# Gathering masked rows for a cumulative sum at the midpoint: a blind front load for every batch, and chunk code entered where the list begins

## The chip, the cores and the metric

The kernel runs on one core of a Trainium2 chip. The metric is the device time of one execution in microseconds (us). A profiled execution also has a span, which runs from the first to the last recorded instruction; the time is a little longer than the span. Engine names are those of the profile: PE (matrix multiply) with PEld (its weight loads), DVE (vector), ACT (scalar), POOL (GpSimd) and SP (sync). A DMA issued from SP or ACT stands in the profile on a queue called hardware_dynamic, one issued from POOL on the queue software_dynamic; a core has 16 DMA engines.

## What is computed

```python
x: [8, 8192, 512] float32, lengths: [8] int64, w: [512, 512] float32
mask = arange(8192) < lengths[:, None]
cs = cumsum(x * mask, axis=1)
mid = cs[b, lengths[b] // 2, :]          # [8, 512]
out = mid @ w                            # [8, 512]
```

So for batch b the kernel needs the sum of the first min(lengths[b] // 2 + 1, lengths[b]) rows of x[b], and then one small matrix product. The lengths are drawn once and fixed: 1138, 5379, 511, 4113, 1809, 7542, 7716, 1140. The rows to be summed are therefore 570, 2690, 256, 2057, 905, 3772, 3859 and 571, which is 14,680 rows of 2 KB, or 30.1 MB out of the 134 MB of x. The lengths are known only when the kernel runs, so it must build the list of what it loads on the chip.

## The kernel before

Rows are handled in groups of U = 4 neighbours (a "quad", 8 KB in one piece). A list of quads runs over all batches, and 128 quads, one per partition, make a chunk of 1 MB. Summing is a matrix product: a weight tile of 128 x 8 zeros and ones says which batch each partition's row belongs to and whether it lies before the end, and four matmuls per chunk (one per row of the quad, each in its own 32-row band of the array, helper `add`, line 285) add into `s_ps`.

**The load without the list.** For batches 0 and 1 the first 512 rows are loaded blind by SP (`xf`, lines 119 to 122), two DMAs of 1 MB whose source is 128 runs of 8 KB in a row. For batches 6 and 7 the first 128 rows come blind, but at the end (`xb`, line 165). Everything else is on the list.

**The list.** DVE (function `vector`; every operation is recorded on line 184 and waits for the one before it) turns the lengths into where each batch's part of the list begins (`row`), PE spreads that over all partitions (line 299 into `bc_ps`), and DVE compares it with each list place to get the quad's number (`idx`). It does this for the first C1 = 8 chunks first (`table(0, C1)`, mark "idx0") and then for the other 57 (`table(C1, C)`, mark "idx"). C = 65 chunks is the most that any lengths could need. The weights `wf`, `wc`, `wb` follow.

**The gathers.** POOL (function `gpsimd`) issues one indirect DMA per chunk (line 151) into a ring of R = 8 buffers `xt`. The code has one block per possible chunk: a compare-and-branch on the list's length (line 171) and the gather, in upward order. Gather c waits for ACT's zeroing of its buffer (`s_zero`; ACT's line 132 clears all eight, since places beyond the list's end are not written) or, from the ninth on, for PE to be done with the buffer (`s_done`). When the list ends, POOL branches to `gp_tail`, which issues the two `xb` and the four `w` loads on the same queue.

**PE** (function `tensor`) does the front, chunk 0, and then a block per chunk: compare-and-branch (line 347), wait for the chunk's semaphore, four matmuls. At the end of the list it branches to `pe_tail`, whose block lies after the blocks of all 65 chunks: the `xb` matmuls, four matmuls that fold the four bands of `s_ps` and transpose (line 331, `mf_ps`), and 16 with w (line 337, `o_ps`). DVE copies between these. SP and ACT each store two pieces of 8 rows of 512 B.

Two waits set the order between the three kinds of work: PE takes the front in order, ahead of every chunk,

```python
for b in range(FRONT):
    pe.wait_ge(s_front[b], 16)      # line 307
```

and a gather beyond the ring waits for PE (`pool.wait_ge(s_done, c - R + 1)`, line 150).

Of the kernel before, what the change touches and what calls it, by code (L numbers as in the profile page):

```python
# [11 lines left out]
P = 128  # L12
# [3 lines left out]
def kernel(  # L16
# [9 lines left out]

    nc = tc.nc
# [7 lines left out]
    FRONT, BACK = 2, 2  # L35
    R0 = [P * U] * FRONT + [0] * (B - FRONT - BACK) + [P] * BACK
    MOST = B * (S // 2 // U + 1)
    C = -(-MOST // P)
    C1 = 8
    FAR = 1 << 17  # L40
    K = [1 - r // U for r in R0]
    JUMP = [UB + (R0[b + 1] - R0[b]) // U - K[b] for b in range(B - 1)] + [FAR]
# [11 lines left out]
    def sem(name):  # L54
        return tc.alloc_semaphore(name)

    xt = sb("xt", [P, R, U * D])
    xf = sb("xf", [P, FRONT, U, D])
    xb = sb("xb", [P, BACK, D])
# [4 lines left out]
    kk = sb("kk", [1, B])  # L64
    negk = sb("negk", [1, B])
    jump = sb("jump", [1, B])
    row = sb("row", [1, 5 * B])
    qk = sb("qk", [1, B])
    mm_ = sb("mm_", [1, B])
    total = sb("total", [1, 1], I32)  # L70
    ones = sb("ones", [1, P])
    zero = sb("zero", [1, D])
    p_i = sb("p_i", [P, 1], I32)
# [6 lines left out]
    f_i = sb("f_i", [P, U], I32)  # L80
    q = sb("q", [P, C])
# [6 lines left out]
    wf = sb("wf", [P, FRONT, U, B])  # L88
    wb = sb("wb", [P, BACK, B])
    fold_i = sb("fold_i", [P, B], I32)  # L90
    fold_m = sb("fold_m", [P, B], I32)
    fold = sb("fold", [P, B])
    s_sb = sb("s_sb", [P, D])
    mf_sb = sb("mf_sb", [P, KC, B])
# [6 lines left out]
    b2_ps = ps("b2_ps", [P, D])  # L101

    s_full = [sem(f"full{k}") for k in range(R)]
    s_front = [sem(f"front{k}") for k in range(FRONT)]
    s_back = [sem(f"back{k}") for k in range(BACK)]
    s_w = [sem(f"w{k}") for k in range(KC)]
    s_len, s_out, s_pool, s_dve, s_pe, s_done, s_zero = (
        sem(n) for n in ("len", "out", "pool", "dve", "pe", "done", "zero"))

    def engine_body(eng, name):  # L110
        eng.br(f"{name}_0")
        return nc.body(f"{name}_0", valid_engines=[eng.engine])

    END = "gather_end"
    bodies = {}


    def sync(sp):
        sp.dma_start(out=xf[:, 0], in_=x[0, :P * U].rearrange("(p u) d -> p u d", u=U)).then_inc(
            s_front[0], 16)  # L120
        sp.dma_start(out=xf[:, 1], in_=x[1, :P * U].rearrange("(p u) d -> p u d", u=U)).then_inc(
            s_front[1], 16)
        sp.wait_ge(s_dve, marks["out"])
        for j in range(0, 4, 2):
            sp.dma_start(out=out[:, j * P:(j + 1) * P], in_=o_sb[32 * j:32 * j + B]).then_inc(s_out, 16)
        sp.wait_ge(s_out, 64)


    def scalar(act):
        act.dma_start(out=lens[:], in_=lens_words).then_inc(s_len, 16)  # L130
        for k in range(R):
            act.memzero(xt[:, k]).then_inc(s_zero, 1)  # L132
        act.wait_ge(s_dve, marks["out"])
        for j in range(1, 4, 2):
            act.dma_start(out=out[:, j * P:(j + 1) * P], in_=o_sb[32 * j:32 * j + B]).then_inc(s_out, 16)


    def gpsimd(pool):
        pool.iota(rank_i[:], pattern=[[0, 1]], base=0, channel_multiplier=13)
        pool.iota(q_i[:], pattern=[[P, C]], base=0, channel_multiplier=0)  # L140
        pool.iota(p_i[:], pattern=[[0, 1]], base=0, channel_multiplier=1)
        pool.iota(v_i[:], pattern=[[P * U, C], [1, U]], base=U, channel_multiplier=0)
        pool.iota(f_i[:], pattern=[[1, U]], base=0, channel_multiplier=U)
        pool.iota(fold_i[:], pattern=[[-1, B]], base=128, channel_multiplier=1).then_inc(s_pool, 1)

        def gather(c):
            if c < R:
                pool.wait_ge(s_zero, c + 1)
            else:
                pool.wait_ge(s_done, c - R + 1)  # L150
            pool.indirect_dma_start(  # L151
                out=xt[:, c % R], out_offset=None, in_=xu,
                in_offset=bass.IndirectOffsetOnAxis(ap=idx[:, c:c + 1], axis=0),
                bounds_check=B * UB - 1, oob_is_err=False,
            ).then_inc(s_full[c % R], 16)

        n = pool.alloc_register("n_pool")
        pool.wait_ge(s_dve, marks["idx0"])
        gather(0)
        pool.load(n, total[:])  # L160
        pool.wait_ge(s_dve, marks["idx"])
        pool.br("gp_1")
        with nc.body("gp_tail", valid_engines=[pool.engine]):
            for k in range(BACK):
                pool.dma_start(out=xb[:, k], in_=x[B - BACK + k, :P]).then_inc(s_back[k], 16)  # L165
            for k in range(KC):
                pool.dma_start(out=wt[:, k], in_=w[k * P:(k + 1) * P]).then_inc(s_w[k], 16)  # L167
            pool.br(END)
        for c in range(1, C):
            with nc.body(f"gp_{c}", valid_engines=[pool.engine]):  # L170
                pool.br_cmp(n, P * c, f"gp_go{c}", "gp_tail", "IS_GT")  # L171
            with nc.body(f"gp_go{c}", valid_engines=[pool.engine]):
                gather(c)
                pool.br(f"gp_{c + 1}" if c + 1 < C else "gp_tail")
# [5 lines left out]
    def vector(dve):  # L180
# [11 lines left out]

        def runs(values):
            k = 0
            while k < len(values):
                e = k
                while e < len(values) and values[e] == values[k]:
                    e += 1
                yield k, e, values[k]
                k = e  # L200
# [4 lines left out]
        for t, values in ((negk, [-a for a in K]), (kk, K), (jump, JUMP)):  # L205
            for k, e, value in runs(values):
                step(dve.memset, t[:, k:e], float(value))
# [3 lines left out]
        step(ts, out=rank4[:], in0=rank_m[:], scalar1=float(U), scalar2=None, op0=ALU.mult)  # L211
        step(ts, out=q[:], in0=q_i[:], scalar1=rank[:], scalar2=None, op0=ALU.add)
        step(ts, out=z[:, :, B], in0=q[:], scalar1=float(R0[0] // U), scalar2=None, op0=ALU.add)
        dve.wait_ge(s_len, 16)
        step(ts, out=l8[:], in0=lens[:, ::2], scalar1=3, scalar2=None, op0=ALU.logical_shift_right)
        step(tt, out=mm_[:], in0=l8[:], in1=negk[:], op=ALU.max)
        step(dve.tensor_tensor_scan, out=row[:, :B], data0=kk[:], data1=mm_[:], initial=0.0,
             op0=ALU.add, op1=ALU.add)
        step(tt, out=row[:, B:2 * B], in0=jump[:], in1=mm_[:], op=ALU.subtract)
        mark("row")  # L220
        step(ts, out=total[:], in0=row[:, B - 1:B], scalar1=0.0, scalar2=None, op0=ALU.add)
        step(tt, out=qk[:], in0=row[:, :B], in1=mm_[:], op=ALU.subtract)
        dve.wait_ge(s_pe, 1)

        def table(a, e):
            n = e - a
            step(tt, out=ge[:, a:e], in0=q[:, a:e].unsqueeze(2).to_broadcast((P, n, B)),
                 in1=bc_ps[:, :B].unsqueeze(1).to_broadcast((P, n, B)), op=ALU.is_ge)
            step(tt, out=z[:, a:e, :B], in0=ge[:, a:e],
                 in1=bc_ps[:, B:2 * B].unsqueeze(1).to_broadcast((P, n, B)), op=ALU.mult)  # L230
            step(dve.tensor_reduce, out=idx[:, a:e], in_=z[:, a:e], axis=AX.X, op=ALU.add)

        table(0, C1)
        mark("idx0")
        step(ts, out=l2[:], in0=lens[:, ::2], scalar1=1, scalar2=None, op0=ALU.logical_shift_right)
        step(dve.scalar_tensor_tensor, out=row[:, 2 * B:3 * B], in0=l2[:], scalar=1.0,
             in1=lens[:, ::2], op0=ALU.add, op1=ALU.min)
        step(tt, out=row[:, 3 * B:4 * B], in0=qk[:], in1=negk[:], op=ALU.add)
        step(dve.scalar_tensor_tensor, out=row[:, 4 * B:], in0=qk[:], scalar=float(U),
             in1=row[:, 2 * B:3 * B], op0=ALU.mult, op1=ALU.add)  # L240
        mark("row2")
        table(C1, C)
        mark("idx")
        step(dve.memset, wf[:], 0.0)
        step(dve.memset, wb[:], 0.0)
        dve.wait_ge(s_pe, 2)
        for b in range(FRONT):
            step(tt, out=wf[:, b, :, b], in0=f_i[:],
                 in1=b2_ps[:, b:b + 1].to_broadcast((P, U)), op=ALU.is_lt)
        mark("front")  # L250

        def weights(a, e):
            n = e - a
            step(tt, out=ge[:, a:e], in0=q[:, a:e].unsqueeze(2).to_broadcast((P, n, B)),
                 in1=b2_ps[:, B:2 * B].unsqueeze(1).to_broadcast((P, n, B)), op=ALU.is_ge)
            step(tt, out=early[:, a:e].rearrange("p c u b -> p (c u) b"),
                 in0=v4[:, a * U:e * U].unsqueeze(2).to_broadcast((P, n * U, B)),
                 in1=b2_ps[:, 2 * B:3 * B].unsqueeze(1).to_broadcast((P, n * U, B)), op=ALU.is_lt)
            step(tt, out=wc[:, a:e], in0=early[:, a:e],
                 in1=ge[:, a:e].unsqueeze(2).to_broadcast((P, n, U, B)), op=ALU.mult)  # L260

# [10 lines left out]
        for k in range(KC):  # L272
            step(dve.tensor_copy, out=s_sb[:, k * P:(k + 1) * P], in_=s_ps[:, k * P:(k + 1) * P])
# [118 lines left out]
```

## Time and profile before

| | us |
|---|---|
| median of 3 runs (97.08 to 97.84) | 97.16 |
| the profiled execution: its time | 97.31 |
| the profiled execution: its span | 95.5 |
| PE / DVE / ACT / POOL busy | 54.1 / 15.9 / 15.8 / 32.6 |
| one gather's issue on POOL (mean of 27) | 1.03 |
| one zeroing of a buffer on ACT (mean of 8) | 1.9 |
| bytes moved by DMA | 31.26 MB, mean 327 GB/s over the span |

The page has a strip of 40 equal slices (2.39 us each) with a digit for how busy each engine and the 16 DMA engines were, and a strip of GB/s. Further views tell the chain of waits that ended last, what single instructions took, and a timeline. The view of windows gives, for any stretch, the busy time of each engine, the granted PE clock, the share of the 16 DMA engines that was busy, and the rate.

### The profile page before, as it was taken

The numbers are of one execution on the slowest core, as the hardware profiler recorded it, in microseconds if no ns is written. First come the engines' busy times: TensorE is split into PE (matmuls) and PEld (weight loads), VectorE is DVE, ScalarE is ACT, GpSimd is POOL, SyncE is SP. The second block draws the span as 40 slices with busy tenths as digits, with TensorE's granted clock in tenths as the row PEclk, the third lists the DMA queues.
The fourth block names the chain that finished last, engine by engine and source line by source line (L and its number), as shares of the span: only waits on it lengthen the run. The fifth ranks groups of instructions, "written<-read, shape, count | busy, mean of one in ns | idle before, by whom it ended". The sixth has DMA issues, their size and how long they took to land.

```text
span 95.5 us, 890 instructions
## 1 busy us (share of the span) xinstructions
PE 54.1 (57%) x308; PEld 8.8 (9%) x308; DVE 15.9 (17%) x56; ACT 15.8 (17%) x9; POOL 32.6 (34%) x43
## 2 busy tenths in 40 slices
PE   2722792447777618763777477746645776219400
PEld 0122100000000000000000000000000000218100
DVE  3778899200000000000000000000000000042100
ACT  3999999200000000000000000000000000000000
POOL 6004578778444440446144534469100000000000
PEclk9999999995555975579556955597596559755555
DMA  2894799999999999999999999999999995000000
GB/s 31 353 412 120 288 353 374 422 425 429 412 436 429 422 401 436 419 412 432 425 412 425 429 412 422 432 412 419 432 422 415 393 389 208 22 0 3 3 10 0
DMA packets 4730, 31.26 MB, mean 327 GB/s; under 512 B 697, under 2 KB 729, under 8 KB 1113
## 3 DMA queue, kind: packets, MB, share of 16 engines
q0 software_dynamic: 4368, 29.04, 74.5%
q1 hardware_dynamic: 320, 2.11, 5.7%
q8 instruction: 5, 0.08, 0.4%
q14 instruction: 3, 0.02, 0.1%
q10 hardware_dynamic: 34, 0.01, 0.0%
HBM read 31.98 MB, written 0.02 MB: 335 GB/s over the span
## 4 chain that ended last, share of the span: by engine, by line
DMA 53%; ACT 17%; PE 12%; issue 9%; DVE 2%; POOL 1%; ACTq 1%; POOLq 0%; SPq 0%
DMA xt<-in_x_dram,idx 53%; ACT xt L132 15%; PE s_ps L286 8%; PE o_ps L337 2%; PE mf_ps L331 2%; ACT L132 1%; DVE s_sb L184 1%; POOL xt L151 1%; ACTq L130 1%; DVE o_sb L184 0%; POOLq L151 0%; POOLq L171 0%; ACTq L387 0%; SPq L46 0%
## 5 line engine op out<-in xcount | busy, mean ns | idle before, releaser
L286 PE MATMUL s_ps<-xt,wc 128*8 128x512 f32 x216 | 42.5, 877 | 24.1 <-DMA xt<-in_x_dram,idx 24.1
L151 POOL DMA_INDIRECT xt<-in_x_dram,idx x27 | 27.7, 1027 | 33.8 <-PE s_ps L286 23.7
L132 ACT ACTIVATE xt<-xt 128x2048 uint32<-128x2048 uint32 x8 | 14.5, 1895 | 0.0
L184 DVE COPY s_sb<-s_ps 128x128 f32<-128x128 f32 x4 | 1.2, 292 | 66.8 <-PE s_ps L286 66.7
L286 PEld LDWEIGHTS s_ps<-xt,wc 128*8 128x8 f32 x216 | 3.4, 89 | 64.0 <-DMA xt<-in_x_dram,idx 62.0
L286 PE MATMUL s_ps<-xf,wf 128*8 128x512 f32 x16 | 3.6, 1051 | 1.7 <-DVE wf L184 1.7
L293 PE MATMUL s_ps<-zero 1*32 1x512 f32 x8 | 1.9, 1056 | 1.9 <-DVE ones L184 1.9
L331 PE MATMUL mf_ps<-fold,s_sb 128*128 128x8 f32 x8 | 1.7, 338 | 2.0 <-DVE s_sb L184 2.0
L286 PE MATMUL s_ps<-xb,wb 128*8 128x128 f32 x16 | 1.0, 410 | 2.6 <-issue 2.6
L184 DVE TENSOR_TENSOR wc<-early,ge 128x256 f32<-128x256 f32 (+1 forms) x2 | 2.5, 1244 | 0.1
L184 DVE TENSOR_TENSOR early<-v,b_ps 128x256 f32<-128x256 f32 (+1 forms) x2 | 2.5, 1237 | 0.1
L167 POOL DMA_DIRECT2D wt<-in_w_dram x4 | 2.2, 575 | 0.0
L331 PEld LDWEIGHTS mf_ps<-fold,s_sb 128*128 128x128 f32 x8 | 1.9, 322 | 2.2 <-issue 1.3
L337 PE MATMUL o_ps<-wt,mf_sb 128*8 128x128 f32 x32 | 1.9, 416 | 0.0
L303 PE MATMUL b_ps<-row,ones 1*128 1x24 f32 x2 | 0.6, 378 | 2.1 <-DVE row L184 2.1
L132 ACT ACT_TABLE_LOAD x1 | 1.3, 1283 | 1.5 <-SPq L46 1.5
L165 POOL DMA_DIRECT2D xb<-in_x_dram x2 | 1.2, 595 | 0.0
L337 PEld LDWEIGHTS o_ps<-wt,mf_sb 128*8 128x8 f32 x32 | 1.1, 126 | 0.4
L299 PE MATMUL bc_ps<-row,ones 1*128 1x16 f32 x2 | 0.6, 380 | 0.8 <-DVE row L184 0.8
L184 DVE COPY mf_sb<-mf_ps 128x8 f32<-128x8 f32 x4 | 0.7, 167 | 1.8 <-PE mf_ps L331 1.8
L184 DVE TENSOR_REDUCE idx<-z 128x8 int32<-128x72 f32 (+1 forms) x2 | 0.9, 459 | 0.1
L184 DVE TENSOR_TENSOR ge<-q,bc_ps 128x64 f32<-128x64 f32 (+1 forms) x2 | 0.9, 426 | 0.4 <-PE bc_ps L299 0.3
(45 smaller groups left out, 12.4 us busy)
## 6 DMA issues: line engine op xcount, KB each, us to landing
xf<-in_x_dram SPq DMA_DIRECT2D x2, 1024.0 KB, 4.9
wt<-in_w_dram POOLq DMA_DIRECT2D x4, 256.0 KB, 15.6
xb<-in_x_dram POOLq DMA_DIRECT2D x2, 256.0 KB, 15.4
xt<-in_x_dram,idx POOLq DMA_INDIRECT x27, 17.2
out_dram<-o_sb SPq DMA_DIRECT2D x2, 4.0 KB
out_dram<-o_sb ACTq DMA_DIRECT2D x2, 4.0 KB
lens<-in_lengths_dram ACTq DMA_DIRECT2D x1, 0.1 KB
```

Source lines behind the costliest of these rows:

```text
L130: act.dma_start(out=lens[:], in_=lens_words).then_inc(s_len, 16)
L132: act.memzero(xt[:, k]).then_inc(s_zero, 1)
L151: pool.indirect_dma_start(out=xt[:, c % R], out_offset=None, in_=xu, in_offset=bass.IndirectOffsetOnAxis(ap=idx[:, c:c + 1], axis=0), boun ...
L165: pool.dma_start(out=xb[:, k], in_=x[B - BACK + k, :P]).then_inc(s_back[k], 16)
L167: pool.dma_start(out=wt[:, k], in_=w[k * P:(k + 1) * P]).then_inc(s_w[k], 16)
L184: do(*args, **kw).then_inc(s_dve, 1)
L286: return pe.matmul(s_ps[32 * j:32 * j + B, cols], lhsT=weights, rhs=rows, start=False, stop=False, skip_group_check=True, tile_position=(0 ...
L293: pe.matmul(s_ps[32 * j:32 * j + 32], lhsT=zero[:, :32], rhs=zero[:], start=True, stop=False, skip_group_check=True, tile_position=(0, 32 ...
L299: pe.matmul(bc_ps[:, :2 * B], lhsT=ones[:], rhs=row[:, :2 * B], start=True, stop=True,).then_inc(s_pe, 1)
L303: pe.matmul(b2_ps[:, :3 * B], lhsT=ones[:], rhs=row[:, 2 * B:], start=True, stop=True, skip_group_check=True).then_inc(s_pe, 1)
L331: pe.matmul(mf_ps[k][:, :B], lhsT=s_sb[:, k * P:(k + 1) * P], rhs=fold[:], start=True, stop=True).then_inc(s_pe, 1)
L337: mm = pe.matmul(o_ps[32 * j:32 * j + B, :P], lhsT=mf_sb[:, k], rhs=wt[:, k, j * P:(j + 1) * P], start=False, stop=(k == KC - 1), skip_gro ...
```

## The change

- **Front.** The first HEAD = 256 rows of every batch are loaded blind, in four DMAs of two batches each (`PAIRS` = 4), all from SP. `xb` is gone. With the drawn lengths the list shrinks from 3353 quads (27 chunks, the last with 25 places filled) to 3161 (25 chunks).
- **List order.** The list is padded at its beginning instead of its end, so that it fills whole chunks: the first 39 places of chunk 0 are empty, and chunk 0 is the last to be taken. Chunks run downward from count - 1 to 0. Only chunk 0's own buffer `xz` is zeroed (one ACT operation instead of eight). All 61 possible chunks' `idx` are made in one go, and all rows of the list's table go through one PE spread of 32 columns instead of two.
- **Branches.** Instead of one compare-and-branch per chunk, POOL and PE each go through a binary tree of compares (`enter`) once, land in the block of the first chunk and run down through the blocks into the tail, which follows chunk 0. In the built program the compares of the tree stand between the chunk blocks. A gather into the ring takes one from a counter `s_free`, which PE's chunks give back.
- **Tail.** w comes in two DMAs with another assignment of rows to `wt` (`QUARTERS`), POOL executes an explicit `drain` after issuing them, the fold makes 32 columns instead of 8, four small matmuls with zero weights take the place of the `xb` matmuls, and SP and ACT store once each, 16 rows of 512 B.

```diff
     def sync(sp):
-        sp.dma_start(out=xf[:, 0], in_=x[0, :P * U].rearrange("(p u) d -> p u d", u=U)).then_inc(
-            s_front[0], 16)
-        ... (the same for batch 1)
-        for j in range(0, 4, 2):
-            sp.dma_start(out=out[:, j * P:(j + 1) * P], in_=o_sb[32 * j:32 * j + B]).then_inc(s_out, 16)
+        for f in range(PAIRS):
+            sp.dma_start(out=xf[:, f],
+                         in_=x[2 * f:2 * f + 2, :HEAD].rearrange("b (q u) d -> b q (u d)", u=U),
+                         ).then_inc(s_front[f], 16)
+        store(sp, 0)
 ...
+    def store(eng, j):
+        eng.wait_ge(s_dve, marks["out"])
+        eng.dma_start(
+            out=out.rearrange("b (j n) -> j b n", n=P)[j:j + 2],
+            in_=o_sb[32 * j:32 * j + 64:4]).then_inc(s_out, 16)
+
+    def enter(eng, name, count):
+        def node(lo, hi, label):
+            with nc.body(label, valid_engines=[eng.engine]):
+                mid = (lo + hi) // 2
+                eng.br_cmp(count, mid, target(mid + 1, hi), target(lo, mid), "IS_GT")
+            for a, e in ((mid + 1, hi), (lo, mid)):
+                if a < e:
+                    node(a, e, target(a, e))
+        ...
 ...
     def scalar(act):
-        for k in range(R):
-            act.memzero(xt[:, k]).then_inc(s_zero, 1)
+        act.memzero(xz[:]).then_inc(s_zero, 1)
 ...
     def gpsimd(pool):
+        pool.wait_ge(s_dve, marks["count"])
+        pool.load(n, count[:])
+        pool.wait_ge(s_zero, 1)
+        enter(pool, "gp", n)
+        for c in range(C - 1, -1, -1):
+            with nc.body(f"gp_c{c}", valid_engines=[pool.engine]):
+                pool.wait_ge(s_dve, marks["idx"])
+                if c:
+                    pool.sem_inc(s_free, -1)._wait_ge(s_free, 1)
+                    gather(xt[:, c % R], c)
+                    pool.br(f"gp_c{c - 1}")
+                else:
+                    gather(xz[:], c)
+                    pool.br("gp_tail")
         with nc.body("gp_tail", valid_engines=[pool.engine]):
-            for k in range(BACK):
-                pool.dma_start(out=xb[:, k], in_=x[B - BACK + k, :P]).then_inc(s_back[k], 16)
+            ... (w in two loads)
+            pool.drain()
 ...
     def tensor(pe):
         pe.wait_ge(s_dve, marks["front"])
-        for b in range(FRONT):
-            pe.wait_ge(s_front[b], 16)
+        for f in range(PAIRS):
+            pe.wait_ge(s_front[f], 16)
             ...
+        pe.wait_ge(s_dve, marks["w"])
+        enter(pe, "pe", n)
+        for c in range(C - 1, -1, -1):
+            with nc.body(f"pe_c{c}", valid_engines=[pe.engine]):
+                pe.wait_ge(s_full[c], 16)
+                ...
+                if c:
+                    mm.then_inc(s_free, 1)
+                pe.br(f"pe_c{c - 1}" if c else "pe_tail")
```

## The prediction

> **What bounds the kernel now.** I read the strips of the page first.
>
> ```profile
> DMA  2894799999999999999999999999999995000000
> GB/s 31 353 412 120 288 353 374 422 425 429 412 436 429 422 401 436 419 412 432 425 412 425 429 412 422 432 412 419 432 422 415 393 389 208 22 0 3 3 10 0
> ```
>
> From slice 7 to 30 the DMA engines are full at about 421 GB/s. There are a hole ahead (slice 3, 120 GB/s) and some 14 us behind in which little moves. The timeline of the full stretch gives the beat:
>
> ```profile
> 24.59 1.89 PE L286 MATMUL s_ps<-xt,wc 128*8 128x512 f32 x8 [0.59 <-DMA xt<-in_x_dram,idx]
> 24.82 0.99 POOL L151 DMA_INDIRECT xt<-in_x_dram,idx  x1 [1.00 <-PE s_ps L286]
> 27.08 1.90 PE L286 MATMUL s_ps<-xt,wc 128*8 128x512 f32 x8 [0.60 <-DMA xt<-in_x_dram,idx]
> ```
>
> A chunk of 128 quads lands every 2.487 us (24.59, 27.08, 29.56). PE needs 1.9 of that and POOL 0.99. Sixteen engines at 8 quads each make 2.487 / 8 = 0.311 us per quad and engine, 26.3 GB/s. The window just before the last w piece lands says that this is an engine's own rate, not a sixteenth of a common one:
>
> ```profile
> 81.00:82.00 1.00, 0.00 (x0) 0.00 (x0) 0.00 (x0) 0.00 (x0) 0.00 (x0) 1.00 0.12 49
> ```
>
> (last two numbers: DMA share, GB/s.) 0.12 of 16 is 1.9 engines, and they move 49 GB/s: 25.5 each. **Few engines are not faster engines.** The end of the chain of waits:
>
> ```profile
> 77.74 2.56 PE s_ps L286 x16
> 80.29 2.60 issue
> 82.89 1.08 PE s_ps L286 x16
> ...
> 85.27 0.62 issue
> 85.89 1.67 PE mf_ps L331 x8
> ```
>
> The 2.60 is a branch: the compare at line 347, 27 times 65 ns but once 3.84 us, at 78.8, where PE leaves the list for its distant tail. The last long thing is a POOL drain of 2.77 us at 91.9.
>
> ```profile
> L347 PEldq COMPARE_BRANCH  x27: 65/65/3840, 13.7 to 78.8; - x27
> ```
> ```profile
> L387 POOLq DRAIN  x3: 46/109/2767, 91.9 to 95.3; - x3
> ```
>
> **The bytes** hardly change. Before: 3353 list quads (27.5 MB), 2.1 MB front, 0.5 MB `xb`, 1.05 MB w, 31.1 in all. After: 3161 quads (25.9), front 4.2, w 1.05, again 31.1. So it matters when, and on how many engines, they move.
>
> **The front load.** Its source is now x[2f:2f+2, :256], 2 batches x 64 quads with 16 MB between the batches, so its outermost extent is 2 and can't be merged with the 64; before, it was 128 quads in a row. What an extent does to the spread is in the queue lines:
>
> ```profile
> q1 hardware_dynamic: 320, 2.11, 5.7%
> ...
> q10 hardware_dynamic: 34, 0.01, 0.0%
> ```
>
> q1 (SP) had two loads of 128 quads and two stores of 8 rows: 272 data packets, 48 over, which is 2x16 + 2x8. q10 (ACT) had the lengths in one piece and two stores of 8: 17 data packets, 17 over, which is 2x8 + 1. One packet over for each engine in use fits all three shapes: 16 engines for extent 128, 8 for 8, 1 for 1. Two readings agree with that: the engines follow the outermost extent, or the rows in all. No DMA of before has two outer dimensions. So the front runs on something from 2 engines to 16, and I keep both ends. I take 2, because the spread seen is a cut along the first dimension and nothing shows a cut along a second.
>
> [...]
>
> On two engines each takes 4 x 64 = 256 front quads instead of 16. The same two must also move their 8 quads of every gather. PE waits for all four fronts before any chunk and frees no buffer meanwhile, so POOL stops after 8 gathers: 64 quads per engine. If the two queues take turns, both are through after 256 + 64 = 320 quads.
>
> The sum, in us of the span. Before, a front issued at 0.96 landed 4.9 later, of which 8 x 0.311 = 2.5 is moving, so start-up is 2.4.
> - Last front lands: 0.96 + 2.4 + 320 x 0.311 = 102.9.
> - PE's matmuls for it: before, two fronts took 3.6; +1.8 = 104.7.
> - PE's entry into the list: a tree of six compares, one of them (25 is not over 30) a jump past some 30 chunk blocks. Priced by the one far jump of before, +3.8 = 108.5. Ends: 0.4 (six at 65 ns) and 7.7 (two far ones).
> - First chunk's matmuls: 1.3 (first chunk before) = 109.8. POOL sees the buffer and issues: 0.8 (PE end 39.85 to issue 40.63) = 110.6. Data flow 1.9 after an issue into an empty queue (issue 7.42, traffic from 9.3) = 112.5.
> - The other 17 gathers, the last with 89 places: 16.7 x 2.487 = 41.5, to 154.0. Landing trails: the first chunk of before took 4.2 from first traffic to PE's wait ending (13.5) where its bytes need 2.5; +1.7 = 155.7.
> - Last matmuls: 78.7 to 80.3 before, 1.6, and four tiny ones with zero weights in place of 1.08 of `xb`: +0.4 (a whole 128-column `xb` matmul lasts 0.41). 157.7. The 2.60 of the far branch is gone, as the tail follows chunk 0.
> - First `s_sb` copy to the end of `o_sb`: 83.99 to 89.74 is 5.75, less 1.26 in which PE's second fold stood in "issue" (84.34 loaded, 85.89 ran): 4.5, 162.2.
> - From there to the end 5.8, less one of two stores per queue (0.4), less 2.7 of drain: 2.7, **span 164.9**. The three drain rows are 2.77, then 0.11 and 0.05 with nothing issued between, so an earlier drain should leave about 0.1. Ends: 0 and 2.7.
> - The profiled execution took 97.31 for a span of 95.5; the 1.8 around it is kept: **166.7**. That execution was 0.15 above the median 97.16, so I say **167**.
>
> **The rest**, costless in this sum, with its cover:
> - Start. DVE loses ten memsets (0.115 apart) and reaches the lengths at 3.0 instead of 4.3; the full `idx` table (three operations of 0.63 to 0.69) comes in one go at about 8.1, where the first 8 columns came at 6.5 and all at 9.3. Cover: the two busy engines until 102.9. Price without it: a later first gather, at most the slack in the second rival.
> - ACT's seven zeroings (13 us) vanish. They held gathers 5 to 8 (issue 15.57, lasting 1.78); gathers now go out every 1.3 but nobody takes them up.
> - `sem_inc` per gather: not in the trace; between 0 and the 1.3 of a whole gather cycle; POOL has 2.49 per chunk, so covered.
> - Strided `s_sb` copies, `mf_sb` 32 wide, weights 32 wide: rows of 0.29 per copy, 0.17 (8 columns) to 0.29 (128), 0.13 (8) to 0.32 (128) per weight load. I take 0; the upper end is some 1.5, as eight groups of weight loads could show.
> - w: 1.05 MB behind the last gather, 2.5 at 421 GB/s; wanted 4 after chunk 0 lands. Covered by 1.5. Stores with outermost extent 2 put 8 rows on an engine, under 0.3.
>
> **Rivals.**
> 1. *The front spreads over all 16 engines: faster.* Fronts land at 0.96 + 2.4 + 32 x 0.311 = 13.3. The first gather goes out at about 9.2 (`idx` at 8.1 + 0.95 as before; POOL's own far jump, from 4.7 to 8.5, is hidden) and has data at 11.1, so the hole closes. Chunk 0 lands at 13.3 + 24.7 x 2.487 = 74.7; + 2.0 + 4.5 + 2.7 + 1.8 = **86**, or 88 if the drain stays. For it: the row-count reading. It decides from 8 engines up: there an engine has 64 front and 198 gathered quads, 3.4 + 262 x 0.311 + 11.0 = 95.9; with 4 it is 115.8 at the least. Chance 0.12.
> 2. *Two engines, but the fronts go ahead of the gathers.* Fronts through at 0.96 + 2.4 + 256 x 0.311 = 83.0. The 8 gathers in the ring then last 20 us, PE frees buffers from 90, so no gap opens: 83.0 + 24.7 x 2.487 = 144.4, + 11.0 = **155**. The trace has no moment with both queues full, so nothing speaks against it but that taking turns is the plainer order. Chance 0.2.
> 3. *The branch and drain edits do not do what they say.* A second code stall on entry or in the tail (3.8) and the drain kept (2.7): 167 + 6.5 = **173**. For it: the fold's 1.26 stall came without any branch just before it. Chance 0.13.
>
> **How the numbers follow.** Forecast 167, chance 0.55. The range 154 to 174 holds the forecast, rivals 2 and 3 and the 1.5 of the weights; rival 1 (0.12) lies outside. Faster by over 1% is rival 1, 0.12; within 1% (about what a measurement of this kernel tells from no change, its runs spreading over 0.8%) would need an engine count that happens to balance, 0.01; slower 0.87.
>
> **What would show it.** Right: four front landings tens of us apart instead of 2.5, the last near 103; a DMA strip at 9 only while the first eight gathers run (to about 31), then at 1 or 2 until past 100, then 9 for some 41 us; about 53 GB/s in the quiet stretch; q1 with some 538 packets (528 data, 8 for four fronts, 2 for a store); PE waiting on the DMA of `xf` for tens of us. Wrong: a strip that is full from slice 1, fronts landed by 14, q1 near 600. Turn-taking is told from rival 2 by when the fourth front lands (103 or 83) and by whether the strip falls to nothing after it. The tail's steps: no "issue" gap over 1 us between the last chunk and `o_sb`, and a last drain of about 0.1.

## The result, and the profile after

The changed kernel takes **178.31 us** (median of 4 runs, 177.83 to 179.0) beside 97.12 for the kernel before on the same chip. The ratio is 1.841, with a 95% interval of 1.828 to 1.854. The predicted sign and cause hold; the size is 11 us more than the 167 I forecast and 4 beyond the end of my range. The profiled execution took 178.0 for a span of 175.9. One kernel below, that with one batch per load, had four of its ten runs in a slower state, the profiled one (99.36) among them, so its time is given as the median of the other six, 97.17, and not of all ten, 98.08.

Strips and queue lines of its page (40 slices of 4.4 us):

```profile
DMA  0159999951111111111111110003999999999800
GB/s 17 56 181 345 335 306 313 311 168 50 56 52 52 54 52 54 52 54 52 54 54 52 54 52 39 4 7 86 360 421 438 421 417 417 429 425 419 366 29 4
...
q1 hardware_dynamic: 538, 4.20, 5.9%
q8 instruction: 5, 0.08, 0.2%
q14 instruction: 2, 0.02, 0.0%
```

The DMA strip is at 9 first while the first eight gathers run, then at 1 from slice 9 to 23, empty for three slices and at 8 or 9 again for ten. q1 has 538 packets: 528 of data, four fronts on two engines (8) and a store on two (2); the DMA share of 0.13 in the windows below is two of 16. But look at the GB/s of slices 3 to 7: 306 to 345, though the digits say 9. Before, from slice 7 to 30, a 9 meant some 421. The windows say the same more sharply (last two numbers: DMA share, GB/s):

```profile
20.00:36.00 16.00, 0.00 (x0) 0.00 (x0) 0.00 (x0) 0.00 (x0) 0.15 (x1) 1.00 1.02 311
40.00:60.00 20.00, 1.36 (x8) 0.00 (x0) 0.00 (x0) 0.00 (x0) 0.00 (x0) 1.00 0.13 53
70.00:100.00 30.00, 3.79 (x16) 0.24 (x16) 0.00 (x0) 0.00 (x0) 0.00 (x0) 1.00 0.13 53
130.00:160.00 30.00, 19.48 (x96) 1.45 (x96) 0.00 (x0) 0.00 (x0) 10.21 (x12) 0.62 1.01 423
```

In the first window all 16 engines are busy and move only 311 GB/s; a gathered quad takes 0.43 us on average in the trace, in place of 0.311. In the second two engines work, alternating between front and gathers (68 front and 69 gathered quads in the trace), in the third two engines on the front alone: 53 GB/s, 26.5 each, 0.311 per quad. In the last, the old rate is back.

Who waited, from the groups of waits:

```profile
POOL xt L159 <- POOLq L174: 110.0, 10, 99.8
PE s_ps L279 <- DMA xf<-in_x_dram: 98.4, 4, 33.5
```

PE waited 98.4 us in all for four front landings (39.33, 70.61, 90.30 and 109.99 in the trace), and POOL stood 99.8 us at one `s_free` (line 174), since PE gives nothing back before it has the front. Two stretches of the timeline, the restart and the beat of the list:

```profile
110.03 1.90 PE L279 MATMUL s_ps<-xf,wf 128*8 128x512 f32 x8 [17.79 <-DMA xf<-in_x_dram]
...
117.15 8.06 PE L279 MATMUL s_ps<-xt,wc 128*8 128x512 f32 x60 [5.23 <-issue]
...
119.97 0.99 POOL L159 DMA_INDIRECT xt<-in_x_dram,idx  x1 [99.82 <-POOLq L174]
...
131.69 1.90 PE L279 MATMUL s_ps<-xt,wc 128*8 128x512 f32 x8 [1.44 <-DMA xt<-in_x_dram,idx]
...
134.18 1.90 PE L279 MATMUL s_ps<-xt,wc 128*8 128x512 f32 x8 [0.59 <-DMA xt<-in_x_dram,idx]
```

The 5.23 of "issue" ahead of the first chunk is the tree of compares, which has two far jumps on PE, of 3.67 and 2.32 us; the branch to the tail is gone. The compares are recorded on line 135 and the drains at the end on line 368 (shortest, median, longest in ns, then the first and last start in us):

```profile
L135 POOLq COMPARE_BRANCH  x6: 34/48/50, 4.8 to 5.8; - x6
L135 PEldq COMPARE_BRANCH  x6: 65/158/3674, 110.3 to 117.0; - x6
```

```profile
L368 POOLq DRAIN  x3: 34/47/178, 174.6 to 175.6; - x3
```

And the end of the chain:

```profile
148.22 18.70 DMA xz<-in_x_dram,idx
166.92 0.04 issue
166.97 1.47 PE s_ps L279 x8
168.44 0.22 PE s_ps L312 x8
168.65 0.02 issue
168.68 0.30 DVE s_sb L195
168.98 0.04 issue
169.02 1.38 PE mf_ps L318 x8
170.41 1.24 PE o_ps L326 x32
171.65 0.02 issue
171.67 0.29 DVE o_sb L195
```

No gap stands between the last chunk and `o_sb`: the fold's old stall and the far branch ahead of it are both gone.

### The profile page after: what moved, and what is told of

Read it like the earlier page. It is cut to its first block, busy times and chain, and to the rows that moved or that the text cites. A ratio compares the mean times of both kernels' runs of the same rounds, so it can differ in the third digit from the quotient of the medians.

```text
span 175.9 us, 843 instructions
## 1 busy us (share of the span) xinstructions
PE 48.7 (28%) x298; PEld 7.4 (4%) x298; DVE 13.7 (8%) x41; ACT 3.2 (2%) x2; POOL 28.3 (16%) x36
## 5 line engine op out<-in xcount | busy, mean ns | idle before, releaser
L159 POOL DMA_INDIRECT xt<-in_x_dram,idx x24 | 24.7, 1031 | 120.9 <-POOLq L174 110.0
L279 PE MATMUL s_ps<-xt,wc 128*8 128x512 f32 x192 | 33.9, 820 | 20.5 <-DMA xt<-in_x_dram,idx 15.3
L279 PE MATMUL s_ps<-xf,wf 128*8 128x512 f32 x32 | 7.6, 1041 | 98.4 <-DMA xf<-in_x_dram 98.4
L195 DVE TENSOR_TENSOR wc<-early,ge 128x1952 f32<-128x1952 f32 x1 | 2.2, 2243 | 0.0
L195 DVE TENSOR_TENSOR early<-v,bc_ps 128x1952 f32<-128x1952 f32 x1 | 2.2, 2186 | 0.0
L121 ACT ACTIVATE xz<-xz 128x2048 uint32<-128x2048 uint32 x1 | 1.9, 1909 | 0.0
L279 PE MATMUL s_ps<-xz,wc 128*8 128x512 f32 x8 | 1.5, 832 | 0.6 <-DMA xz<-in_x_dram,idx 0.6
L318 PE MATMUL mf_ps<-fold,s_sb 128*128 128x32 f32 x8 | 1.4, 286 | 0.4 <-DVE s_sb L195 0.4
L326 PE MATMUL o_ps<-wt,mf_sb 128*32 128x128 f32 x32 | 1.3, 285 | 0.0
L159 POOL DMA_INDIRECT xz<-in_x_dram,idx x1 | 1.0, 987 | 0.3 <-issue 0.3
```

What stands on the lines that cost most here:

```text
L121: act.memzero(xz[:]).then_inc(s_zero, 1)
L159: pool.indirect_dma_start(out=to, out_offset=None, in_=xu, in_offset=bass.IndirectOffsetOnAxis(ap=idx[:, c:c + 1], axis=0), bounds_check=B ...
L195: do(*args, **kw).then_inc(s_dve, 1)
L279: return pe.matmul(s_ps[32 * j:32 * j + B], lhsT=weights, rhs=rows, start=False, stop=False, skip_group_check=True, tile_position=(0, 32 * j))
L318: pe.matmul(mf_ps[k][:, :4 * B], lhsT=s_sb[:, k * P:(k + 1) * P], rhs=fold[:].rearrange("p b r -> p (b r)"), start=True, stop=True).then_i ...
L326: mm = pe.matmul(o_ps[32 * j:32 * j + 32, :P], lhsT=mf_sb[:, k], rhs=wt[:, k, j * P:(j + 1) * P], start=False, stop=(k == KC - 1), skip_gr ...
```

## The experiments

**The engine count.** Four kernels change only the front's source (one also its destination's cut), so that its outermost extent is 64, 4, 8, or, in the kernel before, 2. If the extent sets the engines, the packets and the time follow it.

*One batch per load* (the weights need no change):

```diff
         for f in range(PAIRS):
-            sp.dma_start(out=xf[:, f],
-                         in_=x[2 * f:2 * f + 2, :HEAD].rearrange("b (q u) d -> b q (u d)", u=U),
-                         ).then_inc(s_front[f], 16)
+            for h in range(2):
+                sp.dma_start(out=xf[64 * h:64 * h + 64, f],
+                             in_=x[2 * f + h, :HEAD].rearrange("(q u) d -> q (u d)", u=U),
+                             ).then_inc(s_front[f], 16)
 ...
-            pe.wait_ge(s_front[f], 16)
+            pe.wait_ge(s_front[f], 32)
```

> The changed kernel with each two-batch front load cut into two DMAs of one batch, 64 quads in a row each; nothing else. Theory (the outermost extent 2 holds the front on two DMA engines): eight loads on 16 engines, fronts landed by about 14 us, the strip full from then, last gather landed near 75, and with the tail as the changed kernel's trace has it (166.9 to 175.9, and 2.1 around the span) about 86. Rival (the row count, or the tree of branches and the downward list, make the loss): stays above 150. Beside it: if the 0.41 us quads of the changed kernel between 20 and 38 us come from the order of the list, they are seen here too; if they come from the two busy engines, quads take 0.31 throughout.

Measured: 97.17 (96.82 to 98.24), ratio to the kernel before 1.002 (0.997 to 1.007). The page:

```profile
DMA  1999999999999999998999999999999999960000
GB/s 27 243 216 216 239 219 216 216 219 398 421 418 418 428 408 421 421 364 287 411 432 432 425 425 411 432 421 411 432 425 405 432 428 415 418 280 20 7 3 4
...
q1 hardware_dynamic: 658, 4.20, 19.6%
```

658 is 528 + 8 x 16 + 2: all 16 engines, and the DMA share from 12 to 22 us is 1.01. The 81 us of the change's loss are gone with this one edit, so the engine count is the cause. But the 86 expected of 16 engines missed by 11: while the front runs (slices 2 to 8) full engines move 216 to 239 GB/s, about half of the usual rate. The fronts land at 8.06, 13.10, 17.84 and 23.64. A second, smaller effect must be there.

*Outermost extent 4, and 8* (the same number of bytes, other rows; the weights stay as they are, so the instructions are the same and some rows are summed into the wrong batch):

```diff
-                         in_=x[2 * f:2 * f + 2, :HEAD].rearrange("b (q u) d -> b q (u d)", u=U),
+                         in_=x[4 * (f // 2):4 * (f // 2) + 4, 128 * (f % 2):128 * (f % 2) + 128].rearrange(
+                             "b (q u) d -> b q (u d)", u=U),
```
```diff
+                         in_=x[:, 64 * f:64 * f + 64].rearrange("b (q u) d -> b q (u d)", u=U),
```

> The changed kernel with each front load taking 128 rows of four batches (4 x 32 quads) instead of 256 rows of two; the weights are left, so rows of a wrong batch are summed, the bytes and the work are the same. Theory (engines = outermost extent): four engines with 128 front quads each, queue of 16 + 2 x 4 packets... per load one extra packet for each of 4 engines; fronts landed near 66 to 70, then the changed kernel's own way from the last front to the end (110.0 to 178.0, 68 us): 134 to 138. Rival (a source of several batches 16 MB apart is slow by itself): not faster than 178.

> The changed kernel with each front load taking 64 rows of all eight batches (8 x 16 quads); weights left, as in e2. Theory: eight engines with 64 front quads each, fronts landed near 45, last gather of the ring landed near 51, and 108 to 114 in all. Rival (strided source slow by itself): not faster than 178.

Measured: 154.94 and 131.72 (one run each). The queue lines of the one and of the other:

```profile
q1 hardware_dynamic: 546, 4.20, 8.5%
```
```profile
q1 hardware_dynamic: 562, 4.20, 13.9%
```

528 + 4 x 4 + 2 and 528 + 4 x 8 + 2: four and eight engines; the DMA share from 4 to 9 us is 0.24 and 0.47. Both are some 20 us later than expected. Most of that is the front, whose last load landed at 84.6 and 58.3 us and not near 70 and 45: in these runs a front piece took longer the more engines loaded the front, even before any gather moved data. From 4 to 9 us the mean is 0.309 us with two, 0.41 with four, 0.49 with eight and 0.60 with sixteen engines on 64 partitions.

*The kernel before, its two fronts as 2 x 64 quads* of batches 0 and 1 (weights as they were):

```diff
+        for f in range(2):
+            sp.dma_start(out=xf[:, f].rearrange("p u d -> p (u d)"),
+                         in_=x[0:2, 256 * f:256 * f + 256].rearrange("b (q u) d -> b q (u d)", u=U),
+                         ).then_inc(s_front[f], 16)
```

> The kernel before with one edit: its two front loads take 256 rows of batches 0 and 1 each (2 x 64 quads) instead of 512 rows of one; weights left, so some rows are summed into the wrong batch. Same bytes. Theory: the two loads sit on two engines, 128 front quads and 64 ring quads each, fronts landed near 65 to 70, then the gathers beyond the ring, some 138 to 145 in all. Rival (it is the rest of the change): within 2 us of 97.

Measured: 144.89, fronts at 41.87 and 71.02, q1 292 packets (272 + 2 x 2 + 16: two engines). This one edit of the old kernel costs 48 us, without any of the other edits. It also clears a suspect. In the changed kernel SP was held 32.1 and 32.5 us issuing its third and fourth load; here SP is done at 2.2 us, and yet from 22 to 36 us a gathered quad takes 0.43. The waiting SP isn't what slows the gathers.

**The order of PE's waits.** The front's matmuls go behind the list, into `pe_tail`:

```diff
         pe.wait_ge(s_dve, marks["front"])
-        for f in range(PAIRS):
-            pe.wait_ge(s_front[f], 16)
-            ...
         pe.wait_ge(s_dve, marks["w"])
 ...
         with nc.body("pe_tail", valid_engines=[pe.engine]):
+            for f in range(PAIRS):
+                pe.wait_ge(s_front[f], 16)
+                ...
```

> The changed kernel with its two-engine front as it is, but PE does the front's matmuls after the list instead of before it. Nothing waits for the front until the tail, so the ring never stops. Theory (178 is made of the busy engines' quads plus a stop of the ring that comes from the order of PE's waits): the two engines still carry 256 + 198 = 454 quads; at 0.311 that is 141 us, at 0.41 while the other engines gather more, and the time falls to 157 to 170: the order costs 8 to 20 us, the spread over engines all the rest. Chunks land about 5.2 us apart while the front runs, not 2.5. Rival (it is the order alone that costs, the front running beside): under 120.

Measured: 179.84 (2 runs), ratio to the kernel before 1.847 (1.830 to 1.865). The interval overlaps that of the changed kernel. Windows of this run:

```profile
20.00:40.00 20.00, 5.69 (x24) 0.37 (x24) 0.00 (x0) 0.00 (x0) 3.12 (x4) 1.00 1.01 318
50.00:125.00 75.00, 23.92 (x104) 1.45 (x96) 0.00 (x0) 0.00 (x0) 14.01 (x15) 1.00 0.63 206
130.00:157.00 27.00, 9.47 (x40) 0.59 (x40) 0.00 (x0) 0.00 (x0) 0.00 (x0) 1.00 0.13 53
```

The ring no longer stops, yet nothing is gained: a miss. The two engines have 256 front and 198 gathered quads to move in either order, and their last landing is at 163.9, so that a quad costs them (163.9 - 3.4) / 454 = 0.354. They no longer stand idle between 110 and 122, but as a buffer comes free only when they have done their share (chunks now land some 5.9 us apart), the others gather beside them until 125 us instead of 39, and the slow stretch lasts so much longer. My 157 to 170 took 0.311 for most quads. The order of the waits isn't the cause; the load on two engines is.

**The same bytes on 128 partitions.** Each batch's 256 rows are loaded as 128 partitions x 2 rows, with the weights to match:

```diff
-    xf = sb("xf", [P, PAIRS, U * D])
+    xf = sb("xf", [P, B, 2 * D])
 ...
-        for f in range(PAIRS):
-            ...
+        for b in range(B):
+            sp.dma_start(out=xf[:, b],
+                         in_=x[b, :HEAD].rearrange("(p u) d -> p (u d)", u=2),
+                         ).then_inc(s_front[b], 16)
 ...
+        diag = wf[:].rearrange("p (b e) -> p b e", b=B)
+        step(tt, out=diag[:, :, 0:2 * B:B],
+             in0=f_m[:].unsqueeze(1).to_broadcast((P, B, 2)),
+             in1=rows.unsqueeze(2).to_broadcast((P, B, 2)), op=ALU.is_lt)
 ...
+        for b in range(B):
+            pe.wait_ge(s_front[b], 16)
+            for u in range(2):
+                at = (2 * b + u) * B
+                add((2 * b + u) % 4, wf[:, at:at + B], xf[:, b, u * D:(u + 1) * D])
```

> The changed kernel with its front laid out anew: one load per batch, 256 rows as 128 partitions x 2 rows (4 KB pieces), eight loads; the weights follow, the result is the same. [...] Theory (two engines writing the same partitions halve each other): front pieces take 0.16 us per 4 KB, so 64 of them per engine are through 10.2 us after data starts at 3.4, about 14; then 24.7 chunks x 2.487 from about 15.5 give chunk 0 at 77, and with the measured tail of the changed kernel (167 to 178, 11 us) 88. First gather no later than 14. Rival (a load from SP that spreads over 16 engines is slow by itself, or it is the many loads): pieces take 0.30 us per 4 KB, the front lands at 23 as with one batch on 64 partitions, and the time is 98.

Measured: **89.71** (89.38 to 89.97), ratio to the kernel before **0.922** (0.915 to 0.929), half of the changed kernel's time. The page:

```profile
DMA  1999999999999999999999999999999999981000
GB/s 21 390 259 390 412 420 332 401 363 360 420 416 423 416 427 427 427 420 423 420 423 423 423 427 420 408 420 427 420 420 420 423 431 416 417 348 48 7 6 1
...
q1 hardware_dynamic: 1170, 4.20, 12.9%
```

1170 is 1024 + 16 + 8 x 16 + 2: again 16 engines. Now a 4 KB piece takes 0.159 us (median; the mean is 0.175), the last front lands at 14.26 as expected, and the DMA strip has no hole from slice 1 to 34. This is the version that beats both kernels. Against one batch per load on 64 partitions it differs by the front's layout alone, and by 7.5 us. The layout changes the pieces too, from 8 KB to 4 KB, but here the size of a piece isn't what counts: the front of the kernel before, 8 KB pieces on 128 partitions, took 0.309 us per piece (median). So 16 engines were not enough here: on 64 partitions they took 0.60 us per 8 KB, on all 128 half as much. That two engines were writing the same partitions was my theory; the runs do not show it.

The same without the explicit drain:

```diff
             pool.dma_start(out=wt[:, KC - 1], in_=w[LAST]).then_inc(s_w[1], 16)
-            pool.drain()
             pool.br(END)
```

> As the front on 128 partitions, with POOL's explicit drain after the w loads taken out. Theory (the early drain takes over the waiting that the last instruction otherwise does): the last drain of POOL is 2.8 us instead of under 0.2, and the time is 2.6 us above the one with the drain. Rival (the final drain is short for another reason, such as the two stores): no difference, under 0.5 us.

Measured: 91.38 (90.90 to 91.92), ratio 0.938 (0.930 to 0.946). The longest of the last drains is back:

```profile
L365 POOLq DRAIN  x3: 46/184/2277, 86.2 to 89.4; - x3
```

So the early drain is worth 1.7 us between the medians, 2.2 between the profiled spans, where 2.6 was expected. And the reverse, the kernel before with `pool.drain()` put behind its w loads and nothing else:

> The kernel before with nothing changed but an explicit drain on POOL after the w loads. Theory (the early drain takes over the 2.77 us that the last drain costs): the last drain is under 0.2 and the time 1.7 to 2.7 us lower, 94.5 to 95.5, ratio 0.97 to 0.983. Rival (the last drain costs whatever was drained before): no difference.

Measured: 94.33 (93.95 to 95.12), ratio 0.973 (0.963 to 0.982), which is some 2.7 us:

```profile
L388 POOLq DRAIN  x3: 34/47/109, 91.1 to 92.0; - x3
```

The added drain itself lasts 18.1 us, from 65.8 to 83.9, a little longer than the last w piece needs to land (82.5). It ends before `o_sb` is made, and nothing waits for it. Between the profiled spans the difference is 3.3 us, but 0.8 of it lies ahead of `o_sb`, which is no work of the drain.

**Why quads slow down.** Three kernels load a two-engine front of 80 quads per engine into a few partitions only; PE only waits for it. They are 0 to 7 and 32 to 39 in two of the kernels, 64 to 71 and 96 to 103 in the third; what that does to a gathered quad beside the front is what the runs tell.

```diff
-    xf = sb("xf", [P, PAIRS, U * D])
+    xf = sb("xf", [P, 10, U * D])
 ...
+        for f in range(2):
+            for p in range(4):
+                rows = slice(40 * p, 40 * p + 40)
+                sp.dma_start(out=xf[32 * f + p:32 * f + p + 5:4],
+                             in_=x[2 * f:2 * f + 2, rows].rearrange("b (j u) d -> b j (u d)", u=U),
+                             ).then_inc(s_front[f], 16)
 ...
-        for f in range(PAIRS):
-            ...
+        for f in range(2):
+            pe.wait_ge(s_front[f], 64)
```

> The changed kernel with another two-engine front, of 80 quads per engine: eight loads of 2 x 10 quads, the first batch of a pair into partitions 0-3 and 32-35, the second into 4-7 and 36-39; PE waits for them and leaves the front's matmuls out. Question: why gather quads take 0.41 to 0.43 us between 20 and 35 us while two engines load the front, and 0.311 otherwise. Theory (an engine that writes partitions which other engines are writing slows these): here each front engine writes a few partitions only, so the gather quads of that stretch take 0.31 to 0.34, and the eight gathers of the ring are through on the other engines by 33. Rival (it is the alternation of two queues on two engines, or reading, whatever is written): 0.41 to 0.43 again, through at 38.

Measured: 103.14 (one run). Gathered quads took 0.310 us from 20 to 32 us. But here each partition's 80 KB was contiguous and moved in pieces of 40 KB (1.51 us each), so more than the partitions differed. Hence two more kernels, with pieces of 8 KB, into the same partitions and into those 64 higher (there `at` is 32 * f + p + 64):

```diff
             for p in range(4):
-                rows = slice(40 * p, 40 * p + 40)
-                sp.dma_start(out=xf[32 * f + p:32 * f + p + 5:4],
-                             in_=x[2 * f:2 * f + 2, rows].rearrange("b (j u) d -> b j (u d)", u=U),
-                             ).then_inc(s_front[f], 16)
+                at = 32 * f + p
+                rows = x[2 * f:2 * f + 2, :160].rearrange("b (j p u) d -> p b j (u d)", p=4, u=U)
+                sp.dma_start(out=xf[at:at + 5:4], in_=rows[p]).then_inc(s_front[f], 16)
```

> The changed kernel with a two-engine front of 80 quads per engine into partitions 0-7 and 32-39 as in the run before it, but cut into pieces of 8 KB as in the changed kernel (there a partition's 80 KB lay in one piece of x and moved as 40 KB pieces). PE waits for the front and leaves its matmuls out. Theory (which partitions a front engine writes decides): gather quads between 20 and 33 us take 0.31 to 0.34 again, and twelve or more of a gather's sixteen shares land 2.5 us apart. Rival (it is turn-taking in 8 KB pieces, or reading in 8 KB pieces): 0.40 or more, 3.2 us apart, as in the changed kernel.

> [...] The source and the pieces are the same. [...] Rival (partitions do not matter): the same as with partitions 0-7 and 32-39, landing for landing.

Measured: 109.77 and 118.39 (one run each). The same window of the one and of the other:

```profile
20.00:32.00 12.00, 0.00 (x0) 0.00 (x0) 0.00 (x0) 0.00 (x0) 0.18 (x1) 1.00 1.00 421
```
```profile
20.00:32.00 12.00, 0.00 (x0) 0.00 (x0) 0.00 (x0) 0.00 (x0) 0.17 (x1) 1.00 1.02 298
```

The source, the pieces and the number of front engines (a DMA share of 0.13 from 4 to 9 us in both) are the same; only the partitions written differ, and 421 GB/s become 298. From the trace, for the fifth gather (us; a gather has 16 landings, which I read as one share per engine; the last column is the mean of a gathered quad from 20 to 32 us, in the last row to 36):

| front written to | 1st share lands | 12th | 13th, 14th | last two | a gathered quad |
|---|---|---|---|---|---|
| partitions 0 to 7 and 32 to 39 | 24.73 | 25.52 | 25.57, 25.61 | 38.82, 39.11 | 0.310 |
| partitions 64 to 71 and 96 to 103 | 30.19 | 30.94 | 32.84, 33.19 | 48.88, 48.94 | 0.452 |
| partitions 0 to 127 (the changed kernel) | 26.90 | 28.79 | 28.86, 29.03 | 46.33, 47.81 | 0.429 |

The last two shares are late in every row, as those of two engines with a front to load would be. In the second row two more fall behind the other twelve, by more with each gather (by 3.8 and 4.0 us at the eighth). But the other twelve are slow too: their shares land 3.5 us apart, not 2.48. So the front that went 64 partitions higher held up all sixteen shares of a gather, the 13th and 14th beyond the first twelve. Why these two, no view shows: the trace does not record which engine writes which partitions. A front piece took 0.37 us there (mean from 20 to 32 us).

## Why the prediction was right, and where it was not

**Right.** Two engines ("engines follow the outermost extent"; 538 packets as predicted); turn-taking rather than fronts first (the fourth front landed at 110, not 83, and the last two shares of successive gathers landed 5.2 us apart); the ring that stops after eight gathers; one stretch at 53 GB/s; 2.487 per chunk at the end; the first gather at 9.1 (I said 9.2); the drain and the tail's branch. Against the sum, step by step:

| step of the prediction | predicted us | measured | miss |
|---|---|---|---|
| last front lands | 102.9 | 109.99 | **+7.1** |
| PE's matmuls for it | 1.8 | 1.94 | +0.1 |
| PE's entry into the list | 3.8 | 5.22 | **+1.4** |
| first chunk, POOL's issue | 1.3 + 0.8 | 2.82 | +0.7 |
| data flow after the issue | 1.9 | 1.68 | -0.2 |
| 17 gathers and the landing | 41.5 + 1.7 | 45.27 | **+2.1** |
| last matmuls, dummies | 2.0 | 1.76 | -0.2 |
| `s_sb` to `o_sb` | 4.5 | 3.28 | -1.2 |
| `o_sb` to the end of the span | 2.7 | 3.94 | +1.2 |
| around the span | 1.8 | 2.1 | +0.3 |
| sum | 166.7 | 178.0 | +11.3 |

**The step that failed** is "Last front lands: 0.96 + 2.4 + 320 x 0.311". Its 4 x 64 = 256 front quads per engine put all four loads on the same two engines, which no run of before shows; in the changed kernel the DMA share was two of 16 (0.13 from 4 to 9, from 40 to 60 and from 70 to 100 us) whichever of the loads ran, and the last of them landed at 109.99. The count of 320 is right, its rate isn't while the other engines gather. From 20 to 36 us the two engines moved 38 front quads between them, 19 each, and, taking turns, about as many gathered ones: 16 / 38 = 0.42 us per quad. That lasted from about 11 to 38.7, some 66 quads, and by this estimate 66 x (0.42 - 0.311) = 7.2 us are lost, where 7.1 were missed. What the sum had at nothing is that a two-engine front can slow the gathers beside it, as it did here by the partitions it wrote: the same front left a gathered quad at 0.310 us on partitions 0 to 7 and 32 to 39, and made it 0.452 on 64 to 71 and 96 to 103. The trace of before couldn't show it: there 16 engines loaded each front onto all 128 partitions, at a median of 0.309 us per piece, and the window from which I took "an engine's own rate" had two engines at work and nobody to disturb. I read "few engines are not faster" from it, but not that many could be slower.

The second far jump on entry (3.67 and 2.32, the first of them begun at 110.28 beside the front's matmuls) lay between my ends of 0.4 and 7.7, and was sized by one. The ramp of the second flood of gathers cost 2.1: the first two chunks landed 3.7 apart, 125.46 and 129.16, before the beat of 2.487 set in. The tail's terms cancel each other, which is luck.

**The range** ended at 174 because I let it reach for the rivals and the 1.5 of the weights, and gave the largest term, 320 quads, no upper end of its own. A term of 100 us with a rate from another stretch needs one.

**The rivals.** The first, 16 engines at 86, was wrong in size: one batch per load on 64 partitions gives 97.17, and only all 128 partitions give 89.71; its "decides from 8 engines up" (95.9) fell too, as eight engines give 131.72. The second (fronts first) and the third (branch and drain do nothing) did not occur, apart from the one extra jump.

What the rest of the change is worth can now be told apart: with the front on 128 partitions it takes 7.6 us off the kernel before, of which the drain is 1.7 to 2.2. The front's two-engine load costs the other way 178.31 - 89.71 = 88.6.

## What to carry to other kernels

Look at the outermost extent of a load's source before anything else: here 2, 4, 8 and 64 put the front on 2, 4, 8 and 16 engines, which gave 178, 155, 132 and 97 us for the same bytes, and the packet count of the queue line tells which it was (data packets + engines in use, per load: 538, 546, 562 and 658). Then see how many partitions the load writes: with 16 engines, 128 partitions beat 64 by 7.5 us. Where a few engines carry more than the others, sum their bytes alone, whatever the order of the waits (179.84 us with the front's matmuls last, 178.31 with them first), and don't price a mixed stretch by the rate of a pure one (0.42 us per quad beside 0.311).

## What the runs showed that I had not expected

- **Which partitions a load wrote changed its rate, or that of the gathers beside it.** 16 engines on 64 partitions moved 216 to 239 GB/s, 0.60 us per quad, in place of 0.311. A two-engine front that went 64 partitions higher took a gathered quad from 0.310 to 0.452 us on average, and all sixteen shares were late. That engines which write the same partitions slow each other is a theory that fits both; no run shows the mechanism. Why four engines take 0.41 and eight 0.49, and not double, is left open; so is which resource the engines share.
- **SP was held while it issued loads.** Two loads, each of 64 pieces for each of two engines, went in at 0.7 and 0.5 us; the third and fourth held SP for 32.1 and 32.5; by what, no row shows. It did no harm, as SP had nothing else to do.
- **The two queues did not always take turns.** With one batch per load, where all 16 engines carry the front, the gathers were issued from 13.6 us on, but moved no data before 21.0, when the front was all but through. In the changed kernel the last two shares of the first gather landed at 20.99 and 22.92, while their front ran on to 110. Why they differ is open.
- **The far jumps took longer where the DMA engines were busy.** PE's two took 3.67 and 2.32 us in the changed kernel, with the engines idle (DMA share 0.02 from 110.28 to 117 us), and 6.69 and 5.27 with one batch per load, 5.25 and 5.33 with 128 partitions, where they were full (1.01 from 30 to 38 us in the one, 9 in the strip in the other). The trace tells where the time goes: with each far jump one packet of 16 KB moves on the queue called instruction (q8). From the packet's start to the jump's end it is 2.3 to 2.7 us in all six; what differs is the time before it, 0.96 us and none in the changed kernel, 4.15 and 2.75 with one batch per load, 2.91 and 2.93 with 128 partitions. POOL's first gather is late in the same way: an 8 KB packet on another instruction queue (q14) starts at 5.96, 11.06 and 8.98 us in these three, and the gather goes out at 9.08, 13.59 and 10.99.
- **What the late jumps cost.** With 128 partitions PE reached its first chunk at 26.1 and the ring was refilled from 28.9, in time; with one batch per load it was 36.7 and 39.5, too late, and the strip falls to 364 and 287 GB/s in slices 17 and 18.
